# Products of half the array issued in turn for its two halves in an RWKV chain and its scores, with a new table of priorities

## The chip, the cores and the metric

The kernel runs on one core of a Trainium2 chip. The time is that of one execution on the device, in microseconds (us); of several runs the median counts. A core has a matrix engine (PE, an array of 128 rows by 128 columns), a vector engine (DVE), a scalar engine (ACT), GpSimd (POOL) and a sync engine (SP) that here issues the DMAs. Products go from PE into PSUM, which has eight banks, and DVE or ACT take them from there.

## The reference

One block of a language model: a sequence of 512 tokens, width 1024, all in float32. The normalised input goes through one projection, whose columns feed three mixers; their outputs are joined, projected by `w_out` and added; a feed-forward part with a short convolution follows, and a gated embedding (PLE) at the end:

```python
z = rms_norm(h, pre_mix_norm[i]) @ w_in[i]
o_rw = rwkv7_mixer(token_shift(z_rw, shift_mu[i]), ...)
o_nsa = nsa_mixer(z_nsa, ...)
o_s5 = s5_mixer(z_s5, ...)
mix = jnp.concatenate([o_rw, o_nsa, o_s5], axis=-1).astype(h.dtype) @ w_out[i]
h = h + rms_norm(mix, post_mix_norm[i])
f = conv_ffn(rms_norm(h, pre_ffn_norm[i]), w_up[i], conv_w[i], conv_b[i], w_down[i])
h = h + rms_norm(f, post_ffn_norm[i])
e = rms_norm(p[i] @ w_ple[i], ple_norm[i])
gate = jax.nn.sigmoid((h @ w_ple_gate[i]).astype(jnp.float32)).astype(h.dtype)
h = h + gate * e
```

The change touches the RWKV mixer, which has 6 heads of 64. Each token updates a state `S` of 64 by 64 in each head, and reads its output from it:

```python
def step(S, inp):
    r_t, d_t, k_t, v_t, kk_t, a_t = inp
    sa = jnp.einsum('bhij,bhj->bhi', S, -kk_t)
    S = S * d_t[:, :, None, :] + sa[..., None] * (kk_t * a_t)[:, :, None, :] + v_t[..., None] * k_t[:, :, None, :]
    return S, jnp.einsum('bhij,bhj->bhi', S, r_t)
```

The decay `d` and the rate `a` come from small products (`tanh(wl) @ w2`, `al @ a2`, 64 deep). The NSA mixer is attention in three branches (compressed blocks, selected blocks, a window of 512), with 6 query heads and 2 groups of keys. The S5 mixer is a linear recurrence with complex states.

## The kernel before

**Numbers.** The large products (input, output, up, down, gate) are made of three products each: the operands are split into a high and a low part (`wh`, `wl`, `XH`, `XL` and so on), and high by high, high by low and low by high are added. One such product is 128 deep, 128 wide and 512 long. The products of the recurrence and of the attention probabilities are plain float32; the profile shows two records for each of these.

**RWKV by chunks.** The recurrence is not run token by token. The 512 tokens are cut into 8 chunks `c` of 64. The six heads lie in three groups `f` of two (`hh`).
- `rw_elem(f)` makes decay and rate (the `wa`,`lora` products, 64 deep: the decay's in the upper half of the array's rows, the rate's in the lower), the scaled keys and queries `bk` and `AR`, and the scores between tokens, `AR` by `bk`, which DVE writes under a mask to `AM`. A score product is 64 deep; head `hh` = 0 lies in rows 0 to 63 and `hh` = 1 in rows 64 to 127.
- `rw_inverse` solves the triangular systems in the chunks.
- `rw_chain` then goes over the chunks. For each: `w_of` (the W products, `UV` by `AM`); the product of the state `SS` with `AR`, to which DVE adds W, giving `WU`; the U products (`WU` by `AM`), which ACT copies to `UV`; the BK products (`UV` by `BK`), from which DVE makes the next state; and the output: a product of the state (`SS` by `AR`) and two of `UV` by `AM` for each group. A chunk's products give 64 rows of output, so they use half of the array's columns: an even chunk the first half, an odd chunk the second.
- `rw_out` normalises two chunks' output.

In the kernel before, a chunk's step issues W of the chunk behind it, state, U, BK (three products for the first heads, then three for the second) and its output, one group after the other, each in one half of the columns but BK. In the scores all four products of one head come first, then a DVE multiplication, then the other head.

**What sets the order.** All instructions are recorded through a class `Plan`, so the profile puts all of them on the helper's line, L402 (L406 in the changed kernel). Each part of the work is a stream, a generator that issues instructions and now and then gives way; it has a priority from a table `PR`. `Plan.run` keeps a modelled clock for each engine, takes the engine whose next instruction could start first, and among the streams that could start there within `slack` of it issues the one with the smallest priority value. `_cost` gives the modelled duration of an instruction. So a change in the table or in the costs changes the order in which each engine gets its instructions; that order is fixed when the program is built. Filler for the chain's waits comes from other streams: attention lanes (`nsa`: the `peT`,`V`, `kw`,`q` and `ks`,`q` products, transposes `cf`,`pe`), S5 (`U`,`back`), input projections (`z`).

Streams wait for events and for PSUM banks. Five banks have the tag "z", three the tag "r". `w_out` (in `dense`) goes over four token tiles of 48 products each, and takes two banks for a tile, whose tags stand in `PR["wt"]`. `PR["s5m"]` names an event for which the main S5 stream waits, `PR["nsaev"]` one for some attention lanes, `PR["order"]` the order of the input projections, `PR["mg"]` a margin for waits of PE.

`_cost` before: it keeps a time for each of four column positions until which the array is busy there, and takes products that fill only half of the columns as independent where their columns differ:

```python
before = self.busy[side] if two else max(self.busy.values())
wait = max(0.0, before - t)
if was != mode:
    wait += (190.0 if was[0] != mode[0] else 95.0) * (1.0 if self.warm else 1.5)
```

Of the kernel before, what the change touches and what calls it, by code (L numbers as in the profile page):

```python
# [13 lines left out]
AF = mybir.ActivationFunctionType  # L14
# [5 lines left out]
NT = T // 128  # L20
# [17 lines left out]
NANG = 17 + 64  # L38
NMT = 51
BACC = dict(dynamic_dma_scratch_size=1024)  # L40
PR = {"feed": 78, "order": ["v2", "v1", "r2", "v0", "k0", "r1", "vc", "gl", "k2", "wa", "r0", "k1", "q0", "ks", "kc", "tok0", "kw", "q1", "q2", "u0", "u1", "tok1"], "cmp": -117, "slack": 0, "s5t": 26000.0, "elem": -119, "rw": -111, "s5": -4, "s5o": -210, "nsa": 176, "z": 517, "dense": -75, "evac": 48, "rwo": -71, "pre": 95, "aff": -600, "last": -600, "mix": -35, "zlo": ["dve"], "ple": -330, "lanes": "zzzzrr", "zk": 1, "s5ev": 0, "wt": "zrzr", "pleo": 265, "pt": "zzzz", "s5m": 0, "nsaev": ["at", 2], "sc": "AAD", "nsao": -102, "eT": "AD", "wlo": "POOL", "s5e": "POOL", "rwe": "POOL", "cce": "POOL", "ei": "AAD", "dma0": ["x0", "id", "g", "w0", "x1", "w1", "x2", "co", "x3", "cf"], "ple0": 0, "w3": "POOL", "ms": 0, "s5c": 40, "mg": 0}
NWF = 2
NFF = 8

# [142 lines left out]
class Plan:  # L187
# [8 lines left out]
    def __init__(self, nc):  # L196
        self.clock = {e: 0.0 for e in ENGINES}
        self.clock["HW"] = self.clock["DMA"] = 0.0
        self.hist, self.last, self.base, self.slots, self.ev = {}, {}, {}, {}, {}
        self.streams, self.held, self.tok, self.tokt = [], set(), {}, {}  # L200
        self.now = 0.0
        self.cur = None
        self.set_ = None
        self.warm, self.win, self.cols = False, -TICK / 2, [0.0, 0.0]
        self.side, self.mode, self.busy = None, (128, 128), {0: 0.0, 32: 0.0, 64: 0.0, 96: 0.0}
# [69 lines left out]
    def _cost(self, e, op, out, ins, kw):  # L275

        big = ins[0] if op == "tensor_reduce" else out
        n = 1
        for d in big.shape[1:]:
            n *= d  # L280
        if e == "PE":
            m, k = 1, 1
# [30 lines left out]
            full, c = wait + c, wait + (min(c, (2 * m / 2.4 + 4) * slow) if two else c)  # L313
            if two:
                self.busy[side] = t + full
# [217 lines left out]
def body(nc, tc, ctx, A, dbg=None):  # L533
# [18 lines left out]
    def t2(name, shape=(128, 512), dt=F32):  # L552
        return pl.alloc("t", NMT, tp.tile(list(shape), dt, name=name, tag="t", bufs=NMT))
# [7 lines left out]
    def grab(tag):  # L561

        yield ("tok", tag, 1)
        return pl.hold(ps(tag))
# [736 lines left out]
    def rw_elem(f):  # L1301
# [4 lines left out]
        yield ("ev", "wa")  # L1306
        wa = R["wa"]

        p = yield from grab("r")
        pe.matmul(p, lora[0:64, fs], wa[0:64], start=True, stop=True)  # L1310
        cs = t2("cs")
        act.activation(cs, p, AF.Tanh, scale=0.5, bias=hw[:, f:f + 1])
        drop("r", p)
        p = yield from grab("r")
        pe.matmul(p, lora[64:128, fs], wa[64:128], start=True, stop=True)
        a = t2("a")
        act.activation(a, p, AF.Tanh, scale=0.5, bias=hw[:, 3 + f:4 + f])
        drop("r", p)
# [61 lines left out]
        AM = R["AM"]  # L1380
        m = K("m256")[:, None, :].to_broadcast([128, 2, 256])
        for q in range(2):
            for hh in range(2):
                rr = slice(64 * hh, 64 * hh + 64)
                p = yield from grab("r")
                for i in range(2):
                    for par in range(2):
                        e = slice(2 * par, 2 * par + 2)
                        pe.matmul(p[:, 256 * i + 128 * par:256 * i + 128 * par + 128],
                                  bk[q][rr, i, e].rearrange("p e s -> p (e s)"),  # L1390
                                  R["AR"][f, q][rr, i, e].rearrange("p e s -> p (e s)"), start=True, stop=True)
                u = 4 * hh + 2 * q
                tt(AM[f][:, u:u + 2], p.rearrange("p (i c) -> p i c", i=2), m, op=mul)
                drop("r", p)
                yield "free"
# [108 lines left out]
    def rw_chain():  # L1504
# [8 lines left out]
            for hh in range(2):  # L1513
                pool.memset(SS[q][hs(1 - hh), :, hh], 0.0)

        def w_of(c):

            t, par = divmod(c, 2)
            b = slice(64 * par, 64 * par + 64)
            p_ = yield from grab("r")  # L1520
            p = v4(p_[:, 0:384])
            for f in range(3):
                for hh in range(2):
                    pe.matmul(p[b, f, hh], AM[f][:, 4 * hh + t, 64 + 64 * par:128 + 64 * par], UV[:, c, hh, f],
                              start=True, stop=True)
            W = t2("W", (128, 3, 2, 64)) if c else WU[0]
            copy(W[b], p[b])
            drop("r", p_)
            return W

        W = yield from w_of(0)
        for t in range(NT):
            po = None
            for par in range(2):
                c = 2 * t + par
                b = slice(64 * par, 64 * par + 64)
                al, rt = 1 + par, 3 * par
                Sc, Sn = SS[c % 2], SS[1 - c % 2]
                if c < 7:
                    Wn = yield from w_of(c + 1)  # L1540
                yield
                if c:
                    p_ = yield from grab("r")
                    p = v4(p_[:, 0:384])
                    for f in range(3):
                        pe.matmul(p[b, f], AR[f, t // 2][:, t % 2, al], Sc[:, f], start=True, stop=True)
                    tt(WU[par][b], p[b], W[b], op=add)
                    drop("r", p_)
                    yield
                p_ = yield from grab("r")  # L1550
                pu = v4(p_[:, 0:384])
                for f in range(3):
                    for hh in range(2):
                        pe.matmul(pu[b, f, hh], AM[f][:, 4 * hh + t, 64 + 64 * par:128 + 64 * par], WU[par][:, f, hh],
                                  start=True, stop=True)
                copy(UV[b, c], pu[b].rearrange("p f h i -> p h f i"), scale=-1.0)
                drop("r", p_)
                if 0 < c < 7:
# [4 lines left out]
                if c < 7:  # L1563
                    p_ = yield from grab("r")
                    p2 = p_[:, 0:192].rearrange("p (f i) -> p f i", f=3)
                    for hh in range(2):
                        for f in range(3):
                            pe.matmul(p2[hs(hh), f], BK[f, c // 4][:, c % 4, hs(hh)], UV[:, c, hh, f], start=True, stop=True)
                    for hh in range(2):
                        if c:  # L1570
                            tt(Sn[hs(hh), :, hh], p2[hs(hh)], SD[hs(hh)], op=add)
                        else:
                            dve.tensor_copy(Sn[hs(hh), :, hh], p2[hs(hh)])
                    drop("r", p_)
                if po is None:
                    po_ = yield from grab("r")
                    po = v4(po_[:, 0:384])
                for f in range(3):
                    if c:
                        pe.matmul(po[b, f], AR[f, t // 2][:, t % 2, rt], Sc[:, f], start=True, stop=False)  # L1580
                    for hh in range(2):
                        pe.matmul(po[b, f, hh], AM[f][:, 4 * hh + t, 192 * par:192 * par + 64], UV[:, c, hh, f],
                                  start=(c == 0), stop=(c == 0 or hh == 1))
                if c < 7:
                    W = Wn
            o = t2("o", (128, 3, 2, 64))
            copy(o, po)
            drop("r", po_)
            pl.add(rw_out(t, o), PR["rwo"], pl.end)

    def rw_out(t, o):
        w = slice(128 * t, 128 * t + 128)
# [751 lines left out]
```

## Time and profile before

| what | value |
| --- | --- |
| median of 3 runs | 831.91 us (828.43 to 834.1) |
| profiled execution | 834.77 us, its span 832.8 us, mean PE clock 0.969 |
| PE busy | 788.3 us (95%), 4556 records |
| DVE busy | 505.0 us (61%), 995 |
| ACT busy | 368.6 us (44%), 672 |
| POOL busy | 110.8 us (13%), 129 |
| DMA | 83.05 MB, mean 100 GB/s |
| RWKV chain, first to last output product | 224.1 to 292.7 us |
| end of the attention products | about 404.0 us |

How to read the profile: an instruction stands as engine, line, operation, and tiles as `out<-in`. For a PE product "128*64 128x64" is the part of the array (rows*columns) and the moving operand; "x12" counts records. A time in brackets is idle time ahead of the group and what ended it. Products are pipelined and the ends of the records are modelled, so a group's cost is read from its start to the start of the next. PEclk is the clock that PE was granted, 1.00 being full.

### The profile page before, as it was taken

What the parts mean: (1) busy time and instruction counts of PE and PEld (TensorE: products, weight loads), DVE (VectorE), ACT (ScalarE), POOL (GpSimd) and SP (SyncE); (2) the same over time, 40 slices, a digit from 0 to 9 for tenths busy, and PEclk for the clock granted to TensorE, in tenths of its full rate; (3) what the DMA queues carried; (4) which work ended last, traced back from release to release, by engine and by line L of the source; (5) the groups of instructions that cost most, each with busy time, mean ns of one, the idle gap of its engine ahead of it and who ended that gap; (6) DMA issues with size and microseconds to landing.
All of it is one profiled execution on the core that took longest, in us unless ns stands there. A gap on an engine that the chain in (4) does not pass through costs nothing.

```text
span 832.8 us, 11812 instructions
## 1 busy us (share of the span) xinstructions
PE 788.3 (95%) x4556; PEld 646.7 (78%) x4556; DVE 505.0 (61%) x995; ACT 368.6 (44%) x672; POOL 110.8 (13%) x129
## 2 busy tenths in 40 slices
PE   2998989998999998999999999999999999999998
PEld 1986667786788876777798888888888887888886
DVE  5789686899365766644557665556666554223922
ACT  5333632424664387745435444444444443323511
POOL 2358111000003224710000000000000000000000
PEclk9999996998699998899999999999999999999999
DMA  7212104341026635300222322233322564334111
GB/s 257 89 51 87 42 28 158 126 166 54 15 63 95 186 136 177 102 26 25 77 74 79 101 88 92 100 101 102 102 85 92 177 217 137 102 102 134 43 51 51
DMA packets 37960, 83.05 MB, mean 100 GB/s; under 512 B 7856, under 2 KB 10928, under 8 KB 37904
## 3 DMA queue, kind: packets, MB, share of 16 engines
q1 hardware_dynamic: 37904, 82.30, 30.5%
q8 instruction: 36, 0.59, 0.3%
q14 instruction: 20, 0.16, 0.1%
HBM read 74.42 MB, written 7.86 MB: 99 GB/s over the span
## 4 chain that ended last, share of the span: by engine, by line
PE 72%; DVE 13%; DMA 7%; ACT 4%; issue 2%; POOL 1%; SPq 1%; POOLq 0%; ACTq 0%; DVEq 0%
PE ps L402 72%; DVE wl L402 2%; DMA e<-e2d 1%; DMA wf<-w_out 1%; DMA wf<-w_down 1%; DMA wf<-w_z 1%; DVE Xi L402 1%; DVE tmp L402 1%; DMA ptf<-pT 1%; ACT wh L402 1%; DMA w1c<-w1k 1%; ACT pe L402 1%; SPq L402 1%; DVE XX L402 0%; DVE blk L402 0%
## 5 line engine op out<-in xcount | busy, mean ns | idle before, releaser
L402 DVE TENSOR_TENSOR wl<-wf,wh 128x1024 fp32r<-128x1024 f32 (+2 forms) x92 | 112.0, 1218 | 132.9 <-ACT wh L402 132.6
L402 ACT ACTIVATE wh<-wf 128x1024 fp32r<-128x1024 f32 (+2 forms) x92 | 96.0, 1043 | 117.5 <-PE ps L402 86.2
L402 PE MATMUL ps<-HHL,wh 128*128 128x512 f32 (+1 forms) x352 | 133.6, 380 | 0.3 <-DVE HHL L402 0.3
L402 PE MATMUL ps<-HHH,wh 128*128 128x512 f32 (+1 forms) x352 | 133.7, 380 | 0.3 <-ACT HHH L402 0.3
L402 PE MATMUL ps<-HHH,wl 128*128 128x512 f32 (+1 forms) x352 | 133.5, 379 | 0.0
L402 PEld LDWEIGHTS ps<-HHL,wh 128*128 128x128 f32 x352 | 66.2, 188 | 13.1 <-DVE HHL L402 0.5
L402 PEld LDWEIGHTS ps<-HHH,wh 128*128 128x128 f32 x352 | 66.2, 188 | 13.1 <-ACT HHH L402 0.5
L402 PEld LDWEIGHTS ps<-HHH,wl 128*128 128x128 f32 x352 | 66.2, 188 | 12.3
L402 POOL TENSOR_TENSOR rstd<-rsq_t,mhalf 128x1 f32<-128x1 f32 x20 | 11.8, 592 | 433.2 <-DVE rsq_t L402 429.5
L402 PE MATMUL ps<-XH,wl 128*128 128x512 f32 (+1 forms) x168 | 65.9, 392 | 2.9 <-DVE wl L402 2.9
L402 PE MATMUL ps<-XH,wh 128*128 128x512 f32 (+1 forms) x168 | 67.1, 400 | 0.0
L402 PE MATMUL ps<-wl,GH 128*128 128x512 f32 x168 | 66.1, 393 | 0.7 <-DVE wl L402 0.7
L402 PE MATMUL ps<-XL,wh 128*128 128x512 f32 (+1 forms) x168 | 66.7, 397 | 0.0
L402 PE MATMUL ps<-wh,GH 128*128 128x512 f32 x168 | 65.9, 392 | 0.0
L402 PE MATMUL ps<-wh,GL 128*128 128x512 f32 x168 | 65.8, 392 | 0.0
L402 DVE CUSTOM_DVE_ANT_0 pe<-ps,dtab 128x128 f32<-128x128 f32 (+3 forms) x48 | 22.9, 484 | 28.1 <-PE ps L402 27.8
L402 PEld LDWEIGHTS ps<-XH,wl 128*128 128x128 f32 x168 | 33.2, 198 | 8.6 <-DVE wl L402 3.8
L402 PEld LDWEIGHTS ps<-XH,wh 128*128 128x128 f32 x168 | 33.5, 199 | 6.5 <-issue 1.4
L402 ACT ACTIVATE GH<-cu 128x512 fp32r<-128x512 f32 x22 | 13.9, 631 | 55.0 <-DVE cu L402 55.0
L402 PEld LDWEIGHTS ps<-wl,GH 128*128 128x128 f32 x168 | 31.6, 188 | 8.5 <-DVE wl L402 1.8
L402 PEld LDWEIGHTS ps<-XL,wh 128*128 128x128 f32 x168 | 33.5, 200 | 5.7 <-issue 1.1
L402 PEld LDWEIGHTS ps<-wh,GH 128*128 128x128 f32 x168 | 31.5, 188 | 6.9
(527 smaller groups left out, 1620.9 us busy)
## 6 DMA issues: line engine op xcount, KB each, us to landing
wf<-w_up SPq DMA_DIRECT2D x44, 512.0 KB, 3.4
wf<-w_down SPq DMA_DIRECT2D x22, 512.0 KB, 3.5
wf<-w_z SPq DMA_DIRECT2D x20, 512.0 KB, 3.3
x_t<-x SPq DMA_DIRECT2D x16, 256.0 KB, 3.2
wf<-w_out SPq DMA_DIRECT2D x8, 512.0 KB, 3.8
wf<-w_gate SPq DMA_DIRECT2D x8, 512.0 KB, 3.5
grow<-rows SPq DMA_DIRECT2D x10, 256.0 KB, 5.7
e2d<-e SPq DMA_DIRECT2D x8, 256.0 KB, 2.1
```

The lines of the kernel that those rows point to most:

```text
L402: o.f(*o.args, **kw)
```

## The change

Five things.

1. The table `PR` has new numbers nearly everywhere: priorities of all parts, the order of the projections and of the first loads, the banks of the w_out tiles (z r z r becomes r z r z), the event for S5 (none becomes the first event of "nsa"), the one for the attention lanes, a `slack` of 30 and a margin `mg` of 60, both of which were 0.
2. `_cost` keeps a busy time for eight cells (two halves of the rows by four column positions), so that products in different halves of the rows count as independent too.
3. `rw_elem`: the decay and the rate product of a group are issued one behind the other into two banks, and both tanh follow. The scores of two heads are issued in turn into two banks, two multiplications behind them.
4. `rw_chain`: `w_of(t)` makes W of a pair of chunks, in turn for the even and the odd one, with one copy of 128 rows. The state product of chunk c is issued in turn with the first four output products of chunk c-1, and the U products of c with the other five; these two chunks use different halves of the columns. So the output of a chunk comes a step later, and the loop has a ninth turn for the last.
5. BK of the two heads is issued in turn.

```diff
-PR = {"feed": 78, "order": ["v2", "v1", "r2", ...], "cmp": -117, "slack": 0, "s5t": 26000.0, "elem": -119, "rw": -111, "s5": -4, "s5o": -210, "nsa": 176, "z": 517, "dense": -75, ...}
+PR = {"feed": 109, "order": ["r2", "v1", "v0", ...], "cmp": -166, "slack": 30, "s5t": 28000.0, "elem": -154, "rw": -197, "s5": 5, "s5o": -156, "nsa": 224, "z": 559, "dense": -96, ...}
...
+            part = two or mode[0] < 128
+            at = ins[0].offset // ins[0].ap[0][0]
+            cells = [4 * r + c for r in ((at // 64,) if mode[0] < 128 else (0, 1))
+                     for c in range(side // 32, side // 32 + mode[1] // 32)]
...
-            before = self.busy[side] if two else max(self.busy.values())
+            before = max(self.busy[x] for x in cells)
...
+        yield ("tok", "r", 2)
+        pp = [pl.hold(ps("r")) for _ in range(2)]
+        for i, p in enumerate(pp):
+            pe.matmul(p, lora[64 * i:64 * i + 64, fs], wa[64 * i:64 * i + 64], start=True, stop=True)
...
+            for i in range(2):
+                for par in range(2):
+                    e = slice(2 * par, 2 * par + 2)
+                    for hh in range(2):
+                        rr = slice(64 * hh, 64 * hh + 64)
+                        pe.matmul(pp[hh][:, 256 * i + 128 * par:256 * i + 128 * par + 128],
...
+        def turns_of(*lists):
+
+            n = max(len(l) for l in lists)
+            for i in range(n):
+                for l in lists:
+                    for f in l[i * len(l) // n:(i + 1) * len(l) // n]:
+                        f()
...
+            turns_of(*(amuv(p, c, 64 + 64 * (c % 2), lambda hh, f, c=c: UV[:, c, hh, f]) for c in (2 * t, 2 * t + 1)))
+            W = t2("W", (128, 3, 2, 64))
+            if t:
+                copy(W, p)
+            else:
+                copy(WU[0][0:64], p[0:64])
+                copy(W[64:128], p[64:128])
...
+        def out_of(po, c):
+
+            st = state(po, c, 3 * (c % 2), stop=False) if c else []
+            am = amuv(po, c, 192 * (c % 2), lambda hh, f: UV[:, c, hh, f], start=c == 0, stop=True if c == 0 else None)
+            o = [x for f in range(3) for x in st[f:f + 1] + am[2 * f:2 * f + 2]]
+            return (o[:4], o[4:]) if c else ([], o)
...
+        for c in range(9):
...
+                o1, o2 = out_of(po, c - 1)
...
+                    turns_of(state(p, c, 1 + par), o1)
                     tt(WU[par][b], p[b], W[b], op=add)
...
+                turns_of(amuv(pu, c, 64 + 64 * par, lambda hh, f: WU[par][:, f, hh]), o2)
                 copy(UV[b, c], pu[b].rearrange("p f h i -> p h f i"), scale=-1.0)
...
+                turns_of(*([lambda f=f, hh=hh: pe.matmul(p2[hs(hh), f], BK[f, c // 4][:, c % 4, hs(hh)], UV[:, c, hh, f],
+                                                         start=True, stop=True) for f in range(3)] for hh in range(2)))
```

What this does to PE's order, at three places. First a step of the chain before; `SS`,`AR` are state products, `WU`,`AM` the U products, `UV`,`BK` the next state, `UV`,`AM` W or output, the others filler:

```order
L402 MATMUL ps<-SS,AR 64x128 x3
L402 MATMUL ps<-cf,pe 128x128 x2
L402 MATMUL ps<-kw,q 128x256
L402 MATMUL ps<-kwl,q 128x256
L402 MATMUL ps<-peT,V 64x128
L402 MATMUL ps<-WU,AM 64x64 x6
L402 MATMUL ps<-peT,V 64x128 x3
L402 MATMUL ps<-kw,q 128x256
L402 MATMUL ps<-kwl,q 128x256
L402 MATMUL ps<-U,back 64x64 x6
L402 MATMUL ps<-UV,BK 64x64 x6
```

And now, the end of one step and the beginning of the next:

```order
L406 MATMUL ps<-UV,AM 64x64 x12
L406 MATMUL ps<-kcm,q 128x32 x3
L406 MATMUL ps<-WU,AM 64x64 x2
L406 MATMUL ps<-UV,AM 64x64
L406 MATMUL ps<-WU,AM 64x64
L406 MATMUL ps<-UV,AM 64x64
L406 MATMUL ps<-WU,AM 64x64
L406 MATMUL ps<-SS,AR 64x128
L406 MATMUL ps<-WU,AM 64x64
L406 MATMUL ps<-UV,AM 64x64
L406 MATMUL ps<-WU,AM 64x64
L406 MATMUL ps<-UV,AM 64x64
```

The 12 W products are those of two chunks; the six U products of a chunk stand in turn with five output products of the chunk ahead of it.

Second, where the last attention products (`peT`,`V`) stand to the first three products of a w_out tile (`wh`,`MH`; `wl`,`MH`; `wh`,`ML`). Before, a tile follows on window scores (`kw`,`q`), with attention still to come behind it:

```order
L402 MATMUL ps<-peT,V 64x128 x8
L402 MATMUL ps<-cf,pe 128x128 x4
L402 MATMUL ps<-pcT,vb_115 64x128 x2
L402 MATMUL ps<-gl,g_3042 128x128 x3
L402 MATMUL ps<-kw,q 128x512
L402 MATMUL ps<-kwl,q 128x512
L402 MATMUL ps<-pcT,vb_115 64x128
L402 MATMUL ps<-pcT,vb_116 64x128 x3
L402 MATMUL ps<-kwl,q 128x512
L402 MATMUL ps<-wh,MH_3016 128x512
L402 MATMUL ps<-wl,MH_3016 128x512
L402 MATMUL ps<-wh,ML_3017 128x512
```

Now the first product of the first tile comes behind the last attention product:

```order
L406 MATMUL ps<-cf,pe 128x128 x4
L406 MATMUL ps<-peT,V 64x128 x8
L406 MATMUL ps<-cf,pe 128x128 x3
L406 MATMUL ps<-peT,V 64x128 x7
L406 MATMUL ps<-cf,pe 128x128 x5
L406 MATMUL ps<-peT,V 64x128 x8
L406 MATMUL ps<-wh,MH_2871 128x512
L406 MATMUL ps<-wl,MH_2871 128x512
L406 MATMUL ps<-wh,ML_2872 128x512
```

So no w_out tile stands between attention products any more.

Third, scores (`AR`,`bk`) between input projections (`XH`,`wh` and the like). Before, groups of four for one head:

```order
L402 MATMUL ps<-AR,bk 128x128 x4
L402 MATMUL ps<-XH,wh 128x512
L402 MATMUL ps<-XL,wh 128x512
L402 MATMUL ps<-XH,wl 128x512
L402 MATMUL ps<-XH,wh 128x512
L402 MATMUL ps<-XL,wh 128x512
L402 MATMUL ps<-XH,wl 128x512
L402 MATMUL ps<-XH,wh 128x512
L402 MATMUL ps<-AR,bk 128x128 x4
```

Now groups of eight for both:

```order
L406 MATMUL ps<-AR,bk 128x128 x8
L406 MATMUL ps<-XL,wh 128x512
L406 MATMUL ps<-XH,wl 128x512
L406 MATMUL ps<-XH,wh 128x512
L406 MATMUL ps<-XL,wh 128x512
L406 MATMUL ps<-XH,wl 128x512
L406 MATMUL ps<-XH,wh 128x512
L406 MATMUL ps<-AR,bk 128x128 x8
```

The two heads of a group, which were two groups of four with other work between, are one group in which rows 0 to 63 and rows 64 to 127 take turns.

More of the change, by code (lines that the diff above doesn't have):

```diff
@@ L204, in __init__ @@
         self.warm, self.win, self.cols = False, -TICK / 2, [0.0, 0.0]
-        self.side, self.mode, self.busy = None, (128, 128), {0: 0.0, 32: 0.0, 64: 0.0, 96: 0.0}
+        self.side, self.mode, self.busy = None, (128, 128), [0.0] * 8
         self.port = {"DVE": [], "POOL": []}
@@ L312, in _cost @@
             c *= slow
-            full, c = wait + c, wait + (min(c, (2 * m / 2.4 + 4) * slow) if two else c)
-            if two:
-                self.busy[side] = t + full
+            full, c = wait + c, wait + (min(c, (2 * m / 2.4 + 4) * slow) if part else c)
+            for x in cells:
+                self.busy[x] = t + full
             rest = max(0.0, t + c - self.win - TICK) / c
@@ L1307, in rw_elem @@
         wa = R["wa"]
[L1309 to L1318, printed above, removed]
+        yield ("tok", "r", 2)
+        pp = [pl.hold(ps("r")) for _ in range(2)]
+        for i, p in enumerate(pp):
+            pe.matmul(p, lora[64 * i:64 * i + 64, fs], wa[64 * i:64 * i + 64], start=True, stop=True)
+        cs, a = t2("cs"), t2("a")
+        for i, o in enumerate((cs, a)):
+            act.activation(o, pp[i], AF.Tanh, scale=0.5, bias=hw[:, 3 * i + f:3 * i + f + 1])
+            drop("r", pp[i])
         yield "DVE"
@@ L1520, in w_of, with state @@
+        def state(out, c, row, start=True, stop=True):
+            t = c // 2
+            return [lambda f=f: pe.matmul(out[side(c), f], AR[f, t // 2][:, t % 2, row], SS[c % 2][:, f], start=start, stop=stop)
+                    for f in range(3)]
+        def w_of(t):
             p_ = yield from grab("r")
             p = v4(p_[:, 0:384])
[L1522 to L1525, printed above, removed]
@@ L1541, in rw_chain @@
+        W = yield from w_of(0)
+        po = None
+        for c in range(9):
+            par = c % 2
+            b = side(c)
+            o1, o2 = [], []
+            if c:
+                if po is None:
+                    po_ = yield from grab("r")
+                    po = v4(po_[:, 0:384])
+                o1, o2 = out_of(po, c - 1)
+            if c == 8:
+                turns_of(o1)
+                turns_of(o2)
+            else:
                 yield
@@ L1544, in rw_chain @@
                     p = v4(p_[:, 0:384])
-                    for f in range(3):
-                        pe.matmul(p[b, f], AR[f, t // 2][:, t % 2, al], Sc[:, f], start=True, stop=True)
+                    turns_of(state(p, c, 1 + par), o1)
                     tt(WU[par][b], p[b], W[b], op=add)
                     drop("r", p_)
+                    if par and c < 7:
+                        W = yield from w_of(c // 2 + 1)
                     yield
@@ L1551, in rw_chain @@
                 pu = v4(p_[:, 0:384])
[L1552 to L1555, printed above, removed]
+                turns_of(amuv(pu, c, 64 + 64 * par, lambda hh, f: WU[par][:, f, hh]), o2)
                 copy(UV[b, c], pu[b].rearrange("p f h i -> p h f i"), scale=-1.0)
                 drop("r", p_)
-                if 0 < c < 7:
+            if c and not par:
+                o = t2("o", (128, 3, 2, 64))
+                copy(o, po)
+                drop("r", po_)
+                po = None
+                pl.add(rw_out(c // 2 - 1, o), PR["rwo"], pl.end)
+            if c < 7:
+                Sc, Sn = SS[c % 2], SS[1 - c % 2]
+                if c:
                     SD = t2("SD", (128, 3, 64))
@@ L1562, in rw_chain @@
                 yield
[L1563 to L1578, printed above, removed]
-                    if c:
[L1580 to L1589, printed above, removed]
+                p_ = yield from grab("r")
+                p2 = p_[:, 0:192].rearrange("p (f i) -> p f i", f=3)
+                turns_of(*([lambda f=f, hh=hh: pe.matmul(p2[hs(hh), f], BK[f, c // 4][:, c % 4, hs(hh)], UV[:, c, hh, f],
+                                                         start=True, stop=True) for f in range(3)] for hh in range(2)))
+                for hh in range(2):
+                    if c:
+                        tt(Sn[hs(hh), :, hh], p2[hs(hh)], SD[hs(hh)], op=add)
+                    else:
+                        dve.tensor_copy(Sn[hs(hh), :, hh], p2[hs(hh)])
+                drop("r", p_)
     def rw_out(t, o):
```

38 lines of the change are left out of this document (13 added, 25 removed).

## The prediction, made before the result was known

> **What bounds the kernel now.** I read the page first: how long each engine is busy, the clock, and the chain that ended last.
>
> ```profile
> span 832.8 us, 11812 instructions
> PE 788.3 (95%) x4556; PEld 646.7 (78%) x4556; DVE 505.0 (61%) x995; ACT 368.6 (44%) x672; POOL 110.8 (13%) x129
> PEclk9999996998699998899999999999999999999999
> PE 72%; DVE 13%; DMA 7%; ACT 4%; issue 2%; POOL 1%; SPq 1%; POOLq 0%; ACTq 0%; DVEq 0%
> ```
>
> PE is busy for 95% of the span and carries 72% of the chain; the gaps of the whole run add up to 832.8 - 788.3 = 44.5 us. So PE work that disappears is worth its time, if the work that takes its place is ready. "Busy" does not mean at peak: most of what this change touches fills half of the array. The clock dips in several slices (the line PEclk). Next I cut the span where the change sets in: 203.7 is the start of the inverse, 224.1 the first output product of the RWKV chain, 292.7 its last, 348.7 about the first w_out product, 404.0 the end of attention.
>
> ```profile
> core 0: us, PE busy (x) PEld busy (x) DVE busy (x) ACT busy (x) POOL busy (x), PEclk, DMA share, GB/s
> 203.70:224.10 20.40, 20.40 (x244) 14.94 (x244) 9.26 (x47) 13.39 (x36) 0.96 (x1) 0.54 0.09 29
> 224.10:292.70 68.60, 66.35 (x793) 56.67 (x792) 43.37 (x128) 35.02 (x93) 14.61 (x13) 1.00 0.44 107
> 292.70:348.70 56.00, 49.78 (x277) 37.86 (x277) 37.06 (x122) 44.57 (x101) 28.61 (x30) 0.88 0.42 142
> 348.70:404.00 55.30, 54.46 (x347) 43.49 (x345) 28.92 (x74) 26.39 (x65) 8.40 (x12) 1.00 0.12 39
> 404.00:832.80 428.80, 423.41 (x1992) 353.03 (x1992) 225.43 (x297) 163.23 (x234) 5.50 (x10) 1.00 0.30 101
> ```
>
> The chain's 68.6 us are PE's: it idles for 2.25 of them, at full clock. In the attention behind it (292.7 to 348.7) PE idles for 6.2 us, ACT is busy for 80%, and the clock is 0.88. From 404.0 on it is dense products, which the change only delays or advances.
>
> **Price of a half product.** The timeline of PE, where a row's time to the next row's start is what the group costs (a product in plain f32 leaves two records, so 12 records are 6 products):
>
> ```profile
> 224.10 0.91 PE L402 MATMUL ps<-UV,AM 128*64 128x64 f32 x12
> 224.94 0.33 PE L402 MATMUL ps<-kw,q 128*128 128x128 f32 x1
> 229.65 0.73 PE L402 MATMUL ps<-UV,BK 128*64 128x64 f32 x12
> 230.32 0.33 PE L402 MATMUL ps<-cf,pe 128*128 128x128 f32 x1
> 233.28 0.28 PE L402 MATMUL ps<-cf,pe 128*128 128x128 f32 x1
> 233.48 0.87 PE L402 MATMUL ps<-SS,AR 128*64 128x128 f32 x6
> 234.28 0.33 PE L402 MATMUL ps<-cf,pe 128*128 128x128 f32 x1
> 238.21 0.43 PE L402 MATMUL ps<-SS,AR 128*64 128x128 f32 x2
> ...
> 239.71 0.44 PE L402 MATMUL ps<-cf,pe 128*128 128x128 f32 x2
> 256.07 0.57 PE L402 MATMUL ps<-U,back 128*64 128x64 f32 x12 [1.19 <-DMA back<-away]
> 256.44 0.57 PE L402 MATMUL ps<-UV,BK 128*64 128x64 f32 x10
> 359.55 0.60 PE L402 MATMUL ps<-cf,pe 128*128 128x128 f32 x4
> 362.21 1.09 PE L402 MATMUL ps<-peT,V 128*64 128x128 f32 x16
> 363.24 0.66 PE L402 MATMUL ps<-cf,pe 128*128 128x128 f32 x4
> 373.77 0.39 PE L402 MATMUL ps<-wh__3497,ML 128*128 128x512 f32 x1
> ...
> 377.26 0.39 PE L402 MATMUL ps<-wh__3627,ML 128*128 128x512 f32 x1
> ```
>
> The last two are the first and the last of 16 w_out products in a run: 0.233 apart. All on one half of the columns: 12 records of 64 in 0.84 us, 6 of 128 in 0.80. In turn on both halves: 12 of 64 in 0.37 us (U,back), 31 ns each; 16 of 128 (peT,V) in 1.03, of which the way back to full size is part, so about 57 ns each. The products to BK, three on one half and then three on the other, already overlap in part: 0.67. An exchange between full size and halves: four transposes last 0.60 and one 0.33 (0.28 the shortest), so each further one is 0.09, but from the transpose at 233.28 to the group behind it 0.20 pass: 0.11 to 0.12 each way.
>
> **The chain.** (1) W of two chunks in turn: now 2 x 0.84 = 1.68; then 24 x 0.031 and an exchange and a half = 0.94. Four pairs: -3.0. Their PSUM copies become fewer (eight to five). (2) A step's state products, U products and output products cost 0.80 + 0.84 + (239.71 - 238.21) = 3.14 now. Mixed they are 24 records of 64 and 12 of 128, 24 x 0.031 + 12 x 0.057 = 1.43, with the exchanges about 1.8: -1.35 in each of six steps, -0.75 in the first, which has no state part in its output: -8.9. (3) BK strictly in turn: 0.37 and an exchange, 0.50 against 0.67, seven times: -1.2. Together -13.1. Nothing hides behind this work now (PE idles for 2.25 of 68.6 us), so a gain counts as long as filler is ready.
>
> **Scores and decay products.** These use half of the rows. No row shows row halves strictly in turn.
>
> ```profile
> 89.64 4.80 PE L402 MATMUL ps<-wa,lora 64*128 64x512 f32 x12
> 94.37 0.39 PE L402 MATMUL ps<-CC,bb 128*16 128x128 f32 x2
> 112.73 2.26 PE L402 MATMUL ps<-AR,bk 64*128 64x128 f32 x24
> 115.33 1.16 PE L402 MATMUL ps<-AR,bk 64*128 64x128 f32 x8 [0.33 <-DVE AM L402]
> 125.95 3.09 PE L402 MATMUL ps<-AR,bk 64*128 64x128 f32 x16 [1.28 <-ACT UV L402]
> 130.73 2.07 PE L402 MATMUL ps<-AR,bk 64*128 64x128 f32 x8
> 152.03 1.16 PE L402 MATMUL ps<-AR,bk 64*128 64x128 f32 x8
> 153.11 0.50 PE L402 MATMUL ps<-XH,wl 128*128 128x512 f32 x1
> ```
>
> Scores alone: 8 records in 1.08 us (152.03 to 153.11), 112 ns each and the exchange. 24 in a run take 2.26, 94 ns each: some overlap where one half follows the other. Ends of the range: no gain from turns (0), or both halves for the time of one, 16 in the 1.08 that 8 take. I take the second, since column halves do it (31 against some 60 ns). Twelve groups take 14.6 us now by their rows, about 3.6 of it since 125.95 and 130.73 lie in a half-clock stretch; six groups of 1.08 are 6.5. At full clock that is 14.6 - 3.6 - 6.5: -4.5. If the new place escapes the half clock, another -3.6. The decay and rate products: 12 records in 4.73, then three groups of 4 at two in the time of one and the exchange, 3 x 1.07 = 3.2: -1.5. The Trainium skill, "TensorE: Matmul & The Clock Gate", Part 3 (Measured speedup vs the span model), has four row tiles 3.07 times as fast, not 4 times; two halves at that ratio would be 1.54 times, an estimate from that page by which the scores gain 1.6 us less. No run here shows it, the column rows above (31 ns) are nearer the full factor.
>
> **What the change adds.** In PE's order the exchanges of size rise from 139 to 167. The mixed groups save about 18, so some 46 more lie elsewhere, since other priorities put small fillers between: 46 x 0.115 = +5.3. The new planner costs and the priorities add no instruction; ACT's copies fall by 3. So PE's work: -13.1 - 4.5 - 1.5 + 5.3 = -13.8.
>
> **What is late next.** The order moves more than the chain. Three of the four w_out tiles, 3 x 48 = 144 products, run between the chain's end and the last attention product now, behind 348.7; then all four stand behind the last attention product, and the PLE products go into the chain. Per stretch, with the prices above put on both orders:
> - up to the chain: -1.4 (the -6.0 of scores and decay, against filler that moves here).
> - the chain: priced work 61.5 to 48.5, and the real time stood 7.1 over it; I keep 6.5: 68.6 to 55, -13.6.
> - chain's end to the last attention product: 292.7 to 404.0 is 111.3. After it there are 373 PE, 112 ACT and 174 DVE instructions, against 210, 86 and 123 up to the first w_out product now, which took 56.0 (row 292.70). By PE's priced work it is 59.4, by ACT's count 56.0 x 112/86 = 73, by DVE's 56.0 x 174/123 = 79. PE no longer has w_out products to put between, so what ACT and DVE do in softmax sets the pace: 80. That is -31.3.
> - the rest: w_out's three tiles come here, 144 x 0.233 = 33.5, and small things: +34.4.
>
> Sum -1.4 - 13.6 - 31.3 + 34.4 = -11.9, beside PE's -13.8: two microseconds more idle. The profiled execution took 834.77, the median of the runs is 831.91 (0.9966 of it). 834.8 - 11.9 = 822.9, on the median's scale 820.
>
> **Rivals.**
> - Better (0.17): attention after the chain goes at ACT's 73, and the scores leave the half clock: 820 - 7 - 3.6 = 809; with a chain at 50, 804. For it: in 348.7 to 404.0 PE idles for 0.84 only. Against it: DVE and POOL are denser too.
> - The chain's round trip takes over (0.14). A step needs state product, add, U, copy, BK, add one after the other:
>
> ```profile
> L402 DVE TENSOR_TENSOR SS<-ps,SD 64x192 f32<-64x192 f32 x12 | 4.2, 352 | 4.2 <-PE ps L402 4.1
> L402 DVE TENSOR_TENSOR WU<-ps,W 64x384 f32<-64x384 f32 x7 | 3.9, 556 | 2.3 <-PE ps L402 2.3
> L402 ACT ACTIVATE UV<-ps 64x384 f32<-64x384 f32 x8 | 3.9, 484 | 10.1 <-PE ps L402 10.0
> ```
>
>   0.80 + 0.556 + 0.84 + 0.484 + 0.67 + 2 x 0.352 = 4.05 us, seven times 28. That fits into 55, but DVE (43.4) and ACT (35.0) are busy for half of the chain, and these adds and copies queue behind softmax work. If they cost 2 us more in each step PE has the halves free and nothing to put there: the chain stays at 68.6, 820 + 13.6 = 834. The Trainium skill, "TensorEngine Tiling (Array Packing)", PSUM Bottleneck, warns of that: tiling does not speed up the evacuation.
> - The halves do not overlap as told (0.04): the exchanges remain, +5.3 and 2 of idle, about 839.
> - Slower (0.14): the clock falls.
>
> ```profile
> 325.00:348.00 23.00, 19.52 (x120) 15.04 (x120) 15.13 (x52) 15.29 (x36) 15.69 (x16) 0.71 0.41 144
> ```
>
>   Here PE is busy for 85% at a clock of 0.71. My 80 us of attention have PE work for 59.4, 74%, small products without w_out between. At 0.71 the 59.4 become 83.7, with the same 20.6 of idle 104: +24, 844. From a mean clock of 0.75 in that stretch on it is slower than before by over 1%. Against it: idle is no sure cause, the inverse ran at 0.54 with PE busy for 20.40 of 20.40 us. The Trainium skill, "TensorE: Matmul & The Clock Gate", Part 1, ties the half clock to an idle window of about 3.4 us; by that page alone nothing would fall in a stretch whose gaps are shorter, and the row of the inverse does not agree with it, so I leave the rival its chance.
>
> **How the numbers follow.** Forecast 0.51, 820, own range 808 to 833 (chain 50 to 60, attention 72 to 90). About 1% (823.6 to 840.2) is what a measurement of this kernel can tell from no change. Faster by more than that: 0.38 of the forecast and the better case, 0.55. Same: 0.13 of the forecast, the round trip, and halves without overlap, 0.31. Slower: 0.14. The range 804 to 838 takes in the better case and the round trip, and leaves out the clock and the ends.
>
> **What would show it.** Right: groups UV,AM of 24 records in about 0.8 us and mixed groups SS,AR with UV,AM at under 2.0 us a step; 16 scores in about 1.1; the chain at 50 to 60 us; the first w_out product behind the last peT,V; attention behind the chain at 72 to 90, with ACT and DVE naming PE's gaps. Wrong: a chain near 68 with idle PE released by WU, UV or SS; scores still at 112 ns a record; a clock under 0.75 in attention; or w_out running dry behind attention, for which I have put nothing.

## The result

The changed kernel takes 804.32 us (median of 4 executions, 802.63 to 805.81) against 831.5 for the kernel before: a ratio of 0.967, with a 95% interval of 0.963 to 0.971. The forecast was 820, so the direction was right and the size less than half of what came: -27 us where -12 was expected. 804.32 lies below the forecast's own range (808 to 833) and at the lower edge of the wide one (804 to 838).

The page of the changed kernel, the lines that answer to those of before:

```profile
span 803.8 us, 11825 instructions
PE 766.0 (95%) x4556; PEld 624.0 (78%) x4556; DVE 503.6 (63%) x995; ACT 368.1 (46%) x669; POOL 110.1 (14%) x129
PEclk9999999998999999999999999999999999999999
```

PE is busy for 22.3 us less and idle for 37.8 us instead of 44.5. The line PEclk is the surprise: it shows one dip where before's shows several, and the mean clock went from 0.969 to 0.992.

The same cuts as in the prediction (up to the first product of the chain, the chain, up to the last attention product, the rest), first the one stretch of before that the prediction did not show, then the changed kernel with two more rows for its two falls of the clock:

```profile
core 0: us, PE busy (x) PEld busy (x) DVE busy (x) ACT busy (x) POOL busy (x), PEclk, DMA share, GB/s
0.00:224.10 224.10, 194.33 (x1152) 155.64 (x1153) 170.20 (x378) 99.36 (x183) 53.72 (x64) 0.92 0.30 100
```

```profile
0.00:204.53 204.53, 182.94 (x1180) 148.09 (x1180) 168.32 (x357) 100.64 (x182) 52.24 (x64) 0.98 0.36 118
204.53:263.85 59.32, 56.91 (x644) 44.88 (x644) 35.90 (x139) 36.00 (x92) 0.96 (x1) 0.94 0.33 99
263.85:340.22 76.37, 68.12 (x584) 49.14 (x582) 58.09 (x171) 57.60 (x135) 44.50 (x46) 1.00 0.35 94
340.22:803.80 463.58, 458.05 (x2153) 381.89 (x2152) 241.31 (x330) 173.84 (x264) 12.38 (x18) 1.00 0.30 99
189.00:198.00 9.00, 9.00 (x119) 7.94 (x118) 4.32 (x14) 4.44 (x12) 0.96 (x1) 0.62 0.41 142
216.00:224.00 8.00, 6.07 (x25) 4.63 (x25) 7.30 (x29) 3.35 (x7) 0.00 (x0) 0.59 0.51 164
```

From these rows a table can be made. "Lost clock" is length times (1 - PEclk), with the clock unrounded, and "idle" is length less PE busy; the sums are those of the whole span. Before's chain ends here at its last product (291.8).

| stretch | before | after | difference | forecast | idle before, after | lost clock before, after |
| --- | --- | --- | --- | --- | --- | --- |
| up to the chain | 224.1 | 204.5 | -19.6 | -1.4 | 29.8, 21.6 | 18.8, 3.4 |
| the chain | 67.7 | 59.3 | -8.3 | -13.6 | 2.3, 2.4 | 0, 3.4 |
| to the last attention product | 112.2 | 76.4 | -35.9 | -31.3 | 7.1, 8.3 | 6.8, 0 |
| the rest | 428.8 | 463.6 | +34.8 | +34.4 | 5.4, 5.5 | 0, 0 |
| all | 832.8 | 803.8 | -29.0 | -11.9 | 44.5, 37.8 | 25.6, 6.8 |

The forecast's fourth line held, and its third nearly; the w_out tiles did move behind attention as the order said. Nearly all of what it missed lies ahead of the chain, where it had seen almost no change: there PE idles for 8 us less and loses 15 us less of its clock.

What PE waited for ahead of the chain (waits of PE by what ended them; us in total, times, longest), first before, then after:

```profile
PE ps L402 <- DVE x_t L402: 14.4, 3, 8.3
PE ps L402 <- DVE wl L402: 4.1, 3, 2.0
PE ps L402 <- ACT sq L402: 3.2, 1, 3.2
PE ps L402 <- DVE wer L402: 1.8, 1, 1.8
PE ps L402 <- DVE om L402: 1.4, 1, 1.4
PE ps L402 <- ACT UV L402: 1.3, 1, 1.3
PE ps L402 <- ACT pe L402: 1.1, 1, 1.1
PE ps L402 <- DVE q L402: 1.1, 2, 0.8
```

```profile
PE ps L406 <- DVE x_t L406: 12.9, 3, 9.5
PE ps L406 <- DVE wl L406: 6.8, 5, 2.4
PE ps L406 <- DVE AM L406: 0.9, 1, 0.9
```

The waits for `sq`, and for `q` and `pe`, behind which two of the falls of the clock stood (at 123.4 and 201.9), are gone, and so is the one for `UV`.

The prices of the turns, from PE's timeline of the changed kernel (start, length, group):

```profile
83.41 1.13 PE L406 MATMUL ps<-wa,lora 64*128 64x512 f32 x4
84.47 0.66 PE L406 MATMUL ps<-cf,wei 128*128 128x128 f32 x4
106.52 1.16 PE L406 MATMUL ps<-AR,bk 64*128 64x128 f32 x16
107.61 0.50 PE L406 MATMUL ps<-XL,wh 128*128 128x512 f32 x1
204.53 0.99 PE L406 MATMUL ps<-UV,AM 128*64 128x64 f32 x24
205.45 0.39 PE L406 MATMUL ps<-kw,q 128*128 128x256 f32 x1
224.81 0.27 PE L406 MATMUL ps<-WU,AM 128*64 128x64 f32 x1
...
225.69 0.32 PE L406 MATMUL ps<-cf,pc 128*96 128x128 f32 x1
226.46 0.57 PE L406 MATMUL ps<-UV,BK 128*64 128x64 f32 x12
226.96 0.50 PE L406 MATMUL ps<-PH 128*128 128x512 f32 x1
229.90 0.44 PE L406 MATMUL ps<-SS,AR 128*64 128x128 f32 x4
...
230.72 0.31 PE L406 MATMUL ps<-cf,pc 128*96 128x128 f32 x1
```

W of a pair costs 0.92 (0.94 was forecast), state with output 0.82 and U with output 0.88, together 1.70 (1.8), BK 0.50 (0.50), 16 scores 1.09 (1.08), a pair of decay and rate products 1.06 (1.07).

### The profile page after: what moved, and what is told of

Its sections match the earlier page's. It is cut to its first block, busy times and chain, and to the rows that moved or that the text cites. A ratio compares the mean times of both kernels' runs of the same rounds, so it can differ in the third digit from the quotient of the medians.

```text
span 803.8 us, 11825 instructions
## 1 busy us (share of the span) xinstructions
PE 766.0 (95%) x4556; PEld 624.0 (78%) x4556; DVE 503.6 (63%) x995; ACT 368.1 (46%) x669; POOL 110.1 (14%) x129
## 4 chain that ended last, share of the span: by engine, by line
PE 74%; DVE 13%; DMA 5%; ACT 4%; issue 2%; POOL 2%; SPq 1%; ACTq 0%; POOLq 0%; DVEq 0%
PE ps L406 74%; DVE wl L406 2%; DMA e<-e2d 1%; ACT pe L406 1%; DMA wf<-w_down 1%; DVE tmp L406 1%; DMA x_t<-x 1%; DVE Xi L406 1%; DMA U<-ud 1%; DVE bb L406 1%; SPq L406 1%; POOL rb L406 1%; ACT wh L406 1%; POOL ra L406 0%; DMA back<-away 0%
## 5 line engine op out<-in xcount | busy, mean ns | idle before, releaser
L406 PE MATMUL ps<-XH,wh 128*128 128x512 f32 (+1 forms) x168 | 65.4, 389 | 0.0
L406 PE MATMUL ps<-XL,wh 128*128 128x512 f32 (+1 forms) x168 | 64.5, 384 | 0.4 <-DVE XL L406 0.4
L406 PEld LDWEIGHTS ps<-wh,GL 128*128 128x128 f32 x168 | 31.5, 188 | 6.7
```

Source lines behind the costliest of these rows:

```text
L406: o.f(*o.args, **kw)
```

## The experiments

Two theories were set against each other first. **A**: the turns bring about what was priced, and the rest of the gain is clock and idle time ahead of the chain, which the order of the instructions decides. **B**: the turns save more than the rows showed.

**1. The table alone.** The code of before with the new line `PR`.

```diff
-PR = {"feed": 78, "order": ["v2", "v1", "r2", ...], "cmp": -117, "slack": 0, ...}
+PR = {"feed": 109, "order": ["r2", "v1", "v0", ...], "cmp": -166, "slack": 30, ...}
```

> The code of before with the new table of priorities: nothing is issued in turn, the planner's old costs. Theory A (the order alone removes the half-clock stretches, and these are what the prediction missed): mean clock 0.985 or more, half-clock time under 25 us, and 814 to 820 us, about half of the whole gain. Theory B (what was missed is that turns save more than the rows priced): the table alone brings nothing, 829 to 834 us, clock near 0.97.

Measured: 854 to 869 us in four executions, at clocks of 0.972 to 0.940. They lie too far apart for a ratio, but the fastest of them is slower than any of before. Both theories missed. In its profile, of the slowest execution, 30 us of clock are lost up to the chain and 19 in attention. But the fastest execution had a clock of 0.972, which is that of before, and was still slower by some 20 us; no profile shows why. So the table is no better order in itself; it does not suit the old code and costs.

**2. The code alone.** The new code with the old table, but for one number (`"rwo"`).

> The new code (turns, outputs a step later, new planner costs) with the old table, but for one of its numbers, the priority of the chain's normalised output (-71 to 74), without which the order can't be run. Theory A: the turns bring the priced -13 to -15 us and the clock stays where it was (0.965 to 0.975): 816 to 820 us. Theory B: 806 to 812 us at an unchanged clock.

Measured: 825.66 us, a ratio of 0.993 (0.989 to 0.996), clock 0.974. The clock stayed as theory A had it, but the gain was half of the priced one, so the time lies outside both ranges. The windows show where it went:

```profile
0.00:198.52 198.52, 168.54 (x1036) 134.92 (x1037) 159.60 (x324) 85.16 (x148) 51.49 (x63) 0.92 0.31 105
198.52:248.73 50.21, 50.21 (x637) 39.22 (x636) 35.35 (x144) 30.84 (x88) 0.31 (x1) 1.00 0.11 33
248.73:356.51 107.78, 96.38 (x739) 73.69 (x735) 71.16 (x197) 76.72 (x172) 50.97 (x50) 0.97 0.47 139
```

Up to the chain and in the chain it is ahead of the full change (248.7 against 263.9), with a chain without any idle time. But PE does less other work in that time, and the attention left over then takes 107.8 us, 11.4 of them idle, where the full change needs 76.4.

**3. No turns, the same order.** The planner plans the new kernel as it is; only when the products of a group are issued, those of one half all come first. The order of the other engines is the same, instruction by instruction.

```diff
-            for i in range(n):
-                for l in lists:
-                    for f in l[i * len(l) // n:(i + 1) * len(l) // n]:
-                        f()
+            turns = [f for i in range(n) for l in lists for f in l[i * len(l) // n:(i + 1) * len(l) // n]]
+            pl.one_half_first(turns, [f for l in lists for f in l])
...
+    def one_half_first(self, turns, halves):
...
+        for o, x in zip(take(halves), take(turns)):
+            x.args, x.kw = o.args, o.kw
+            self.cur.q.append(x)
```

> The new kernel, the order of every engine kept, but within each group of the chain and of the scores the products of one half all come first, then those of the other (the decay and rate products stay as they are, the output still comes a step later). By the prices of the rows: W +2.6, state, U and output +8.4, BK +1.2, scores +4.3, together +16: 817 to 822 us if PE's work is all that counts. Theory B: +25 or more. A rival (the chain waits for its adds and copies, so its products are partly hidden): +8 or less, under 813 us.

Measured: 808.66 us, 0.972 (0.969 to 0.976): only 3 to 4 us slower than the changed kernel. That is the rival's case, and theory B falls. PE's timeline shows one reason:

```profile
202.01 1.43 PE L420 MATMUL ps<-UV,AM 128*64 128x64 f32 x24
203.37 0.39 PE L420 MATMUL ps<-kw,q 128*128 128x256 f32 x1
```

12 products on one half with 12 records each, one half behind the other, cost 1.36 us, not the 2 x 0.84 of two lone groups. An estimate: by the prediction's 0.11 to 0.12 for an exchange each way, one exchange less saves about 0.23 of these 0.32 us; the rest would be overlap where the second half follows the first. Summed over all groups (from a group's start to the next, idle time left out) the chain's products take 31.6 us before, 29.3 in this run, 22.7 in the changed kernel; the scores 14.9, 10.4 and 7.45. So the turns themselves save 9.5 us of PE. The run without turns has the higher clock (0.998): in its profile one fall did not occur, and the other lasted half as long. With that taken off ("What lost clock costs" has the rate) the turns bring about 6 us of time. The rest is hidden: without turns PE idles for 34.7 us, 3.1 less than in the changed kernel.

**4. Work in the idle gap ahead of a fall, in the kernel before.**

```diff
         p = yield from grab("r")
+        R["nsq"] = R.get("nsq", 0) + 1
+        if R["nsq"] == 3:
+            pl.pre = [(p, ident, cf[:, 0:512])] * 3
         for t in range(NT):
             pe.matmul(p[:, 2 * t:2 * t + 2], sq[:, 128 * t:128 * t + 128], K("hind"), start=True, stop=True)
```

`pl.pre` holds products that are issued right ahead of the next one, without the planner's knowledge, so nothing else moves.

> The kernel before with three idle full-size products (128x512, into a bank that is written again right behind them) ahead of the last squared-norm products, where PE idles for 3.24 us at 118.5 before its clock falls at 123.4. They add about 2.6 us of work into the idle time and nothing else moves. Theory A (the gap makes the clock fall, and the 17 us at half clock cost PE time): the stretch 123 to 140 runs at clock 1.00, mean clock 0.98, and the time falls by 6 to 9 us, to 823 to 826. Rival (the other engines set the pace of that stretch, so clock there costs nothing): within 2 us of before. Rival (the clock falls for another cause than the gap): the stretch stays at 0.50.

Measured: 828.98 us, 0.995 (0.992 to 0.998). The place before (first two lines: the wait, and the window that holds the fall), then with the work in the gap:

```profile
121.72 0.83 PE L402 MATMUL ps<-cf,sq 128*128 128x2 f32 x6 [3.24 <-ACT sq L402]
116.00:142.00 26.00, 21.38 (x99) 16.36 (x98) 20.29 (x45) 9.44 (x15) 2.99 (x3) 0.67 0.24 84
```

```profile
118.41 2.84 PE L405 MATMUL ps<-cf 128*128 128x512 f32 x6
121.78 0.83 PE L406 MATMUL ps<-cf,sq 128*128 128x2 f32 x6 [0.52 <-ACT sq L406]
```

```profile
116.00:142.00 26.00, 21.70 (x123) 15.09 (x122) 23.41 (x52) 10.88 (x18) 2.98 (x3) 1.00 0.27 96
```

The wait shrinks from 3.24 us to 0.52, and the clock that was 0.50 from 123.4 to 140.5 is 1.00. So the gap does make it fall here. The time fell by 4, about half of what was expected, and the whole lost clock by less than the 8.5 us of this stretch: the profile has 19.5 us of it against 25.6 before, with another fall at 78.0 to 81.4. At the rate of 0.58 found below, these 6.1 us are worth 3.5.

**5. The old planner costs** with the new code and table.

```diff
-            before = max(self.busy[x] for x in cells)
+            before = max(self.busy[x] for x in (cells if two else range(8)))
...
-            for x in cells:
+            for x in cells if two else ():
```

> The new kernel, planned with the old costs (only products in different columns count as independent, not those in different rows); code and table are the new ones. Theory A (the gain beyond the turns comes from an order that fits this table, these costs and this code together): another order, more half-clock time and more idle, 812 to 840 us. Theory B (the costs are a refinement): 802 to 808 us.

Measured: 846.37 us, 1.020 (1.015 to 1.026): slower than the kernel before and above the range of theory A too, though every turn is there. The chain's products take 23.4 us and the scores 9.3 (22.7 and 7.45 in the changed kernel); what differs most is the order, and with it the clock (0.960) and PE's idle time:

```profile
0.00:202.91 202.91, 168.86 (x1045) 133.53 (x1045) 160.87 (x332) 89.02 (x154) 51.44 (x63) 0.93 0.31 105
202.91:257.05 54.14, 53.32 (x603) 40.35 (x602) 23.13 (x66) 21.55 (x52) 0.83 (x1) 0.89 0.17 59
257.05:391.56 134.51, 118.59 (x808) 89.87 (x806) 79.90 (x271) 84.89 (x206) 48.63 (x50) 0.91 0.36 111
```

Idle 34.1, 0.8 and 15.9 us, lost clock 14.7, 5.8 and 12.0.

**6. Only the chain without turns.** As the third, with the scores in turn.

> As the run without turns (808.7 us), but only the chain's products are taken one half after the other; scores stay in turn. The two traces so far have the chain's products at 29.3 us of PE against 22.8, the scores at 10.4 against 7.45. If PE time counts in full: the chain's turns are two thirds of the difference, 806.5 to 807.5 us. If the chain's turns are hidden: 804 to 805. If the scores' are: 808 to 809.

Measured: 806.43 us, 0.971 (0.966 to 0.977), between the two, at the edge of the first expectation. Its chain products take 28.7 us, its scores 7.46. The differences of one to two microseconds are at the limit of what these runs can tell.

**7. The old order of the input projections**, all else new: one entry of the table.

```diff
-"order": ["r2", "v1", "v0", "vc", "k0", "r1", "gl", "v2", "k2", "wa", "r0", "k1", "kc", "q0", "kw", "q1", "ks", "tok0", "u0", "u1", "tok1", "q2"]
+"order": ["v2", "v1", "r2", "v0", "k0", "r1", "vc", "gl", "k2", "wa", "r0", "k1", "q0", "ks", "kc", "tok0", "kw", "q1", "q2", "u0", "u1", "tok1"]
```

> The new kernel with the old order of the input projections in the table, all else new. Theory A (the order sets where PE runs dry ahead of the chain, and so the clock): idle and lost clock ahead of the chain rise from 21.6 and 4.1 us to over 28 and over 10, and the time to 812 to 830. Rival (the code's turns make the chain's inputs ready early whatever the order): under 808.

Measured: 833.34 us, 1.002 (0.998 to 1.005): with this one entry the whole gain is gone, more than theory A expected. The entry moves the planned order as a whole, so it is not the projections alone that are tested.

```profile
0.00:214.53 214.53, 184.26 (x1132) 148.62 (x1132) 167.09 (x372) 95.88 (x174) 49.45 (x63) 0.92 0.30 102
214.53:264.47 49.94, 49.94 (x646) 38.74 (x647) 30.72 (x123) 29.06 (x85) 0.00 (x0) 1.00 0.26 66
264.47:401.82 137.35, 121.56 (x790) 92.14 (x786) 75.59 (x194) 75.78 (x172) 54.91 (x54) 0.94 0.32 107
```

Idle ahead of the chain is 30.3 us and lost clock 17.1, near those of the kernel before (29.8 and 18.8). The chain takes 49.9 us, less than in the changed kernel, and ends at nearly the same time (264.5 and 263.9). PE has issued fewer other products by then, 1778 records against 1824, and the time comes back as attention, of 137.4 us with three w_out tiles in it.

**8. The gap ahead of the changed kernel's last fall.** In the state group of chunk 2 PE issues one output product and then waits 1.93 us for the state; the clock falls in that wait, at 217.4. Two products go in there.

```profile
218.40 0.45 PE L406 MATMUL ps<-SS,AR 128*64 128x128 f32 x1 [1.93 <-DVE SS L406]
```

```diff
+            def one(f):
+                if c == 2 and f == 0 and stop:
+                    pl.pre = [(out.rearrange("p a b c -> p (a b c)"), ident, cf[:, 0:384])] * 2
+                pe.matmul(out[side(c), f], AR[f, t // 2][:, t % 2, row], SS[c % 2][:, f], start=start, stop=stop)
+            return [lambda f=f: one(f) for f in range(3)]
```

> The new kernel with two idle products (128x384, into the state's bank, written again behind them) in the 1.93 us at 216.4 in which PE waits for the state before its clock falls at 217.7. Theory A: that fall goes, the lost clock time drops by 2.5 to 3.5 us and the time by 1.5 to 3, to 801 to 803 us. Rival (a fall costs nothing in the chain, whose steps wait anyway): 804 to 805, or slower by the work added.

Measured: 799.78 us, 0.964 (0.959 to 0.969), the lowest of all. Since the fall at 190 was missing in its profile too, it was run again beside the changed kernel itself:

> The new kernel itself, beside the one with the filled gap, so that the two are compared on one chip: 802 to 806 us, clock 0.989 to 0.995.

> The new kernel with the gap at 216.4 filled, again. Theory A (the fall at 217.7 is gone in each execution): clock 0.994 to 0.999, 1.5 to 3 us less than the new kernel beside it. If the 4.5 us of the first look were mostly the chance fall at 190 that was missing there: under 1 us less.

Measured: 805.83 us (801.06 to 806.45) for the changed kernel and 803.03 (802.41 to 804.73) with the gap filled, six executions each; the ratios to before, 0.966 (0.962 to 0.970) and 0.965 (0.961 to 0.968), overlap. The window of the fall, first the changed kernel, then with the gap filled:

```profile
216.00:224.00 8.00, 6.05 (x25) 4.61 (x25) 7.30 (x29) 3.35 (x7) 0.00 (x0) 0.59 0.52 164
```

```profile
216.00:224.00 8.00, 7.64 (x58) 5.15 (x57) 7.74 (x30) 4.84 (x11) 0.00 (x0) 1.00 0.60 193
```

The fall is gone, and the chain's stretch goes from 59.3 to 57.0 us. But the clock of the six lay between 0.991 and 0.994, hardly the expected 0.994 to 0.999: the profile has falls at 166.0 and 316.2 that the changed kernel's lack, and loses 6.8 us of clock in all, where the two of the changed kernel lose 6.8 and 8.5. All ten executions with the gap filled have a median of 802.6, the ten of the changed kernel 805.6. So by the medians this version is the fastest, by some 3 us, with ranges that overlap in the last comparison.

**What lost clock costs.** Beside these runs stand 41 executions of the kernel before. Its order is the same each time, and yet its clock lay between 0.964 and 0.981, lost clock of 15.8 to 30.1 us. The times go with it: a straight line through the 41 rises by 0.58 us for each microsecond of lost clock (correlation 0.78). That it is less than 1 would fit stretches in which PE waits for other engines anyway; no run shows it. The Trainium skill, "TensorE: Matmul & The Clock Gate", Part 1, has the gate at 4/8 after an idle window of about 3.4 us; the fall here at 123.4 in the kernel before came 1.7 us behind a gap of 3.24 us, and that at 217.4 in the changed one 0.9 us into a gap of 1.93 us, so idle time below that window was enough, with small products beside it. The trace does not agree with the page, and the measurement goes for this kernel.

The traces show two things more. Between the first and the last change of the clock, every stretch at half or full clock in the twelve profiles is a whole multiple of 3.41 us long. And in the 3.41 us ahead of each of the 45 falls (those at the very end of a span left out) PE idles for 0.30 to 3.19 us, so none needed a whole such stretch without work. The 0.30 us stand ahead of the changed kernel's fall at 190.1, where PE is at work, in part on products of 32x32: not each fall has a gap that could be filled.

## Why the prediction was off

Point by point, by its own steps:

- **The prices of the turns held.** W 0.92 against 0.94, a mixed step 1.70 against 1.8, BK 0.50, scores 1.09 against 1.08, decay and rate 3.2. For the halves of the rows, of which no row of before spoke, the end that was taken (two in the time of one) was right. The ratio for row tiles of the Trainium skill, "TensorE: Matmul & The Clock Gate", Part 3 (3.07 for four), carried over to two halves as an estimate of 1.54, does not agree with the trace: 16 records take 1.09 us where 8 on one half took 1.08.
- **What they replace was priced too high in the chain.** The step "a step's state, U and output products cost 3.14 now", taken for all chunks with the W and BK prices (eight times W, U and output, seven times state and BK), makes 35.7 us; all groups of before together took 31.6. Lone groups were priced, while in before's order W of one chunk stood beside the output of another in three places (groups of 23, 16 and 16 records), and these overlap already, as here in before:

```profile
231.17 1.55 PE L402 MATMUL ps<-UV,AM 128*64 128x64 f32 x23
232.51 0.32 PE L402 MATMUL ps<-peT,V 128*64 128x128 f32 x1
```

  23 records in 1.34 us, where two lone groups of 12 make 1.68. The term was -13.1 and measured 22.7 - 31.6: -8.9.
- **Scores and decay: -6.0 forecast, -9.0 measured** (14.9 to 7.45 and 4.7 to 3.2). The better case's -3.6 for the half clock is in it: the scores did escape it.
- **The step that failed is "up to the chain: -1.4".** It carried two assumptions that were not priced: that the idle time and the half-clock stretches ahead of the chain stay, and that only the scores could leave them. The order of before holds 51 us at half clock, 38 of them ahead of the chain, and the sum kept them all; the only place where the prediction let the clock move for the better was the better case, with 3.6 us. In fact 18.8 us of lost clock went (15.4 ahead of the chain), by the rate of 0.58 about 11 us of time, and 6.7 us of idle (8.2 ahead of the chain) where +2 was forecast. 29.0 = about 11 (clock) + 6.7 (idle) + about 11.4 (PE's work), and the last stands beside the forecast's 13.8. The split is an estimate, but it also fits the runs that have all the turns and another order. Their profiles are longer than the changed kernel's by 15.9 us (code alone), 27.0 (old projection order) and 40.6 (old costs); idle time and 0.58 of the lost clock make 15.8, 24.2 and 33.8 of that.
- **Attention and the rest** were right in their numbers: 76.4 against 80, and +34.8 against +34.4. But the mechanism of the first was only in part: the step had PE at work for 59.4 of the 80 us and idle for 20.6, with ACT and DVE setting the pace. PE was busy for 68.1 and idle for 8.3, of which ACT's results ended 3.9 and DVE's 3.8. That the sum of the two came near is partly luck.
- **The rivals.** The round trip of the chain did not take over (2.4 us of idle in 59.3). The fall of the clock in attention did not come (1.00), though falls of the clock decided much of the result ahead of it. In the attention of the runs with the old costs and the old projection order the clock is 0.91 and 0.94, with 12.0 and 8.5 us lost, but there one and three w_out tiles stand between, so that is not the rival's case. The run of the code alone, without w_out tiles there, has 0.97. The time came out at the 804 of the better case, and by chance: that one had the chain at 50 us and attention at 73, where they took 59.3 and 76.4.

What stays open: why this order has so few falls, and what decides whether a short gap makes the clock fall. The exchanges of size, forecast at +5.3, were not measured by themselves. And which of the table's other entries matter was not tried, but for the projections.

## What to carry to other kernels

Price a regrouped product from what its neighbours cost in the old order, not from lone groups, and check the price by summing all groups of its kind. Where an order is planned, a change of a cost or of one table entry moves far more than the edited lines: the same turns gave 0.967, 1.002 and 1.020 of the old time with three orders. And look for each fall of the clock in the old profile, find the gap ahead of it, where there is one, and ask whether the new order still has that gap; some work in a gap that a wait leaves anyway can be worth more than it costs (some 4 and 3 us in the two trials here).

## What the runs showed of the hardware

Row halves in turn run fully side by side here: 16 score records in 1.09 us against 8 in 1.08. One half behind the other costs less than two lone groups: 24 W records took 1.36 us, against 2 x 0.84 alone and 0.92 in turn. The smallest products hardly gain by the full clock: a group of 16 products of 32x32 (32 records) took 1.02 us at a clock of 0.50 (203.75 to 204.77 before) and 1.00 at full clock (187.07 to 188.07 after):

```profile
203.75 1.10 PE L402 MATMUL ps<-T,AM 32*32 32x32 f32 x32
204.77 0.80 PE L402 MATMUL ps<-XH,wl 128*128 128x512 f32 x1
```

```profile
187.07 1.08 PE L406 MATMUL ps<-T,AM 32*32 32x32 f32 x32 [0.30 <-DVE T L406]
188.07 0.40 PE L406 MATMUL ps<-wl,XH 128*128 128x274 f32 x1
```
